# Values of 64-wide heads in two passes, a reordered opening, and projections spread over the heads' turns

## The chip, the cores and the metric

The kernel runs on one core of a Trainium2 chip. The metric is the device time of one execution in microseconds (us): the median of three timed executions. A separate execution was recorded by the hardware profiler; all rows and all times of single instructions here come from it. In the profile PE is the matrix engine TensorE, PEld its weight loads, DVE the vector engine, ACT the scalar engine, POOL the GpSimd engine and SP the engine that issues most loads.

## The reference, cut to what matters

Two transformer blocks run one after the other on a sequence of 512 tokens of width 1024, in float32. The first has two layers (latent attention, then sparse attention, each followed by cross attention and a feed-forward network); the second has forgetting attention beside a pooling mixer, and a convolutional feed-forward network. The change touches the first attention of the first block (16 heads) and the attention of the second block (8 heads). Both have heads of 64 values:

```python
h = x @ w_in                                  # 512 + 256 + 32 columns
q = (rms_norm(c_q, q_norm) @ w_uq)            # per head 64 plain + 32 rotated
kv = (rms_norm(c_kv, kv_norm) @ w_ukv)        # per head 64 key + 64 value
k = concat([k_nope, broadcast(apply_rope(k_rope))])
out = dense_causal_attention(q, k, v, (MLA_NOPE + MLA_ROPE) ** -0.5)
...
s = einsum('bqhd,bkhd->bhqk', qi, k32)        # second block, 8 heads of 64
s = s + Fi[..., None] - Fk[:, :, None, :]
p = softmax(where(qpos >= kpos, s, -inf))
o = einsum('bhqk,bkhd->bqhd', p, v32)
```

## The kernel before, in words

Products keep float32 accuracy by splitting each operand into a high part (rounded to the reduced type fp32r) and a low part (the rest). `split` (lines 157 to 165) makes them with one ACT copy and one DVE subtraction; `mm3` (lines 151 to 155) multiplies high by high, high by low and low by high, three passes on PE into one accumulator. Weights are loaded by SP as "units" in a fixed order (`plan`), and `use` prepares units ahead of their use: ACT makes the high part (L121), and DVE, or POOL during attention, the low part (L122).

**The opening** (`mla`, from line 482). Four tiles of 128 tokens of x are transposed on PE (`tr`, L509) and multiplied by the eight units of the first projection (`front`, 24 pairs of products for each tile, written to `pa` and `pb`). `norm` scales the rows on DVE, `back` transposes them again (L553). SP issues the loads in the order: first halves of x, the first units, then `setup` (nine small loads of constants), then tiles 2 and 3 of x. After the fourth tile the rotated query parts are projected into four accumulators `rq` (two groups of 48 products of 256 columns, one before and one after `back(3, ...)`), rotated by `rope` on DVE (POOL does the products of the later three), values of the first eight heads are projected (`vproj(0)`, four tiles of six products each), and `proj(0)` projects keys (six products) and queries (12 products) of the first two heads. The rotated rows are copied into place by loads on ACT's queue, L622, L623 and L636.

**Attention** (`attention`, lines 672 to 744) runs a loop of turns. In turn h PE multiplies values by probabilities for head h-3 (`s3`, 12 products into `o`), transposes the probabilities of head h-2 (`s2`, ten transposes into three accumulators `t`, which ACT and DVE split into `pt`), and computes the scores of head h (`s1`, 12 products into `s`). DVE subtracts the row maximum and masks (L692), ACT exponentiates (L694); `norm` scales head h-1 on POOL with four instructions (L703). Then `ahead(h)` and `fill(h)` put other PE work into the turn: in even turns the key and query projections of the pair of heads after next (18 products, 4.1 us), in turns 0, 4 and 8 a whole rotation, in turns 1, 3 and 4 the values of the second eight heads (`FILL_V`), and from turn 8 on steps of the cross attention's keys and values (`FILL_A`). Odd turns without a fill have scores, transposes and values alone.

The value product of a head is

```python
o = self.ps("o")
for j in range(NT):
    self.mm3(o[0:64, 128 * j:512], [v[j][:, 0], v[j][:, 1]], [pt[j][:, 0], pt[j][:, 1]], j == 0, j == 3)
self.split(OT[h // 2][r, 0], OT[h // 2][r, 1], o[0:64])
```

with 512, 384, 256 and 128 columns of probabilities for j = 0 to 3 and 64 columns of values as the stationary operand. The second block calls the same `attention` with 8 heads and a lag of 4 turns; there the low parts of weights are made on DVE, and the last four turns have no projection in them.

The order on each engine is a list made before the run, in which an instruction whose inputs are expected early may stand before one that is written earlier. Each engine works through its own list in order.

Of the kernel before, what the change touches and what calls it, by code (L numbers as in the profile page):

```python
# [35 lines left out]
FILL_V = {1: (0,), 3: (1,), 4: (2, 3)}  # L36
# [28 lines left out]
class K:  # L65
# [416 lines left out]
    def mla(self):  # L482
# [3 lines left out]
        for t in range(NT):  # L486
# [8 lines left out]
            if t == 1:  # L495
                self.setup(last)
# [20 lines left out]
        def front(ts, then=None):  # L517
            xT = [x0T.pop(t) if t in x0T else tr(t) for t in ts]
            pp = [(self.ps("pa"), self.ps("pb")) for _ in ts]
            for k in range(8):  # L520
                if len(us) == k:
                    us.append(self.use(3))
                u = us[k]
                for x, (pa, pb) in zip(xT, pp):
                    l = [x[0][:, k], x[1][:, k]]
                    self.mm3(pa, l, [u[0][:, 0:512], u[1][:, 0:512]], k == 0, k == 7)
                    self.mm3(pb[:, 0:288], l, [u[0][:, 512:800], u[1][:, 512:800]], k == 0, k == 7)
                if k == 4 and then is not None:
                    x0T[then] = tr(then)
# [50 lines left out]
        uu = [self.use(), self.use()]  # L580
        for m in range(4):
            rps.append(self.ps("rq"))
        for g in range(2):
            if g == 1:
                back(3, prev)
# [6 lines left out]
            if g == 0:  # L592
                st = {n: self.use() for n in ("v", "k", "q")}
        V = {}

        def vproj(h, js=range(NT)):
            if h == 1 and js[0] == 0:
                st["v"] = self.use()
            u = st["v"]
            for j in js:  # L600
                p = self.ps("v")
                c = slice(j * 128, j * 128 + 128)
                for k in range(2):
                    self.mm3(p, [x[:, c] for x in ckvs[k]], [u[0][:, k], u[1][:, k]], k == 0, k == 1)
                V[h, j] = self.pair("v")
                self.split(V[h, j][:, 0], V[h, j][:, 1], p)

        kr = self.pair("kr")
        self.rope(krf, kr, nc.vector)
# [3 lines left out]
        def ropes(m):  # L613
            rq = self.pair("rq")
            self.rope(rsb[m], rq, nc.vector if m == 0 else nc.gpsimd)
            ropeq.append(rq)
        nc.scalar.copy(rsb[0], rps[0])
        ropes(0)
        for m in range(1, 4):
            nc.scalar.copy(rsb[m], rps[m])  # L620
        for i in range(2):
            nc.scalar.dma_start(KF[i][0][64:96].bitcast(F), kr[64:96].bitcast(F))  # L622
            nc.scalar.dma_start(KF[i][1][32:64].bitcast(F), kr[32:64].bitcast(F))  # L623
        OT = []
        vproj(0)

        def proj(p):
            if p == 4:
                st["k"] = self.use()
            if p in (2, 4, 6):  # L630
                st["q"] = self.use()
            ring = p % 2
            for hd in range(2):
# [3 lines left out]
            for src, nk, w, cc, dst in ((ckvs, 2, st["k"], (p % 4) * 128, KF), (cqs, 4, st["q"], (p % 2) * 128, QF)):  # L637
# [1065 lines left out]
```

## Time and profile before

| | |
|---|---|
| median of three timed executions | 2175.67 us (2175.51 to 2180.46) |
| profiled execution, its time | 2170.42 us |
| its span, first to last instruction | 2168.6 us |
| PE busy | 2125.2 us, 98% of the span |
| DVE, ACT, POOL busy | 61%, 43%, 13% |

Busy shares are means over stages with different limits, so the stages that the change touches are read by themselves below: the opening and first attention (0 to about 230 us of the span) and the second block's attention (about 1677 to 1765 us). A line of the timeline gives the start, the time from start to end, the engine, the line of the kernel, what is written and read, the shape, how many are merged, and in brackets the idle time before it and what ended it. Products on PE overlap, so what one costs is the distance from its start to the next one's start, not its own time.

### The profile page before, as it was taken

Reading aid. Unit: us, or ns where it says so; the run is one execution under the profiler, and the core shown is the slowest. Engines: PE = TensorE matmul, PEld = TensorE weight load, DVE = VectorE, ACT = ScalarE, POOL = GpSimd, SP = SyncE. Lnnn points to the kernel's source line nnn. Section 1 sums busy time; section 2 is a strip of 40 time slices with the busy share of each in tenths; the row PEclk is TensorE's granted clock in tenths of the full one; section 3 lists DMA queues with packets and bytes.
Section 4 is the critical chain, followed back from the end, with each engine's and each line's share of the span. In section 5 each row is a group of like instructions: output and inputs, shape, how many; then the busy total and the mean of one; then the engine's idle time right before and its main releaser. Section 6 shows DMA issues by size and latency. Waiting matters only on the chain.

```text
span 2168.6 us, 30013 instructions
## 1 busy us (share of the span) xinstructions
PE 2125.2 (98%) x11492; PEld 1776.7 (82%) x11492; DVE 1324.1 (61%) x2747; ACT 925.7 (43%) x1684; POOL 287.9 (13%) x288
## 2 busy tenths in 40 slices
PE   8999999999999999899999999999999999999998
PEld 7789898988888887775688888888888879888886
DVE  6776566735237267877676845446377677755734
ACT  3687444313225143578734332224224655343521
POOL 0255100000000002476300000000004310000002
PEclk9999999999999999999999999999999999999999
DMA  6123613355324132240332345444320335432311
GB/s 209 49 67 99 205 59 117 96 167 155 97 94 151 54 107 65 77 123 27 125 119 79 117 155 184 136 127 159 104 59 21 88 112 156 146 94 91 126 59 39
DMA packets 254178, 233.82 MB, mean 108 GB/s; under 512 B 14516, under 2 KB 219700, under 8 KB 254036
## 3 DMA queue, kind: packets, MB, share of 16 engines
q1 hardware_dynamic: 246384, 214.19, 32.1%
q10 hardware_dynamic: 7652, 17.73, 2.6%
q8 instruction: 90, 1.47, 0.3%
q14 instruction: 52, 0.43, 0.1%
HBM read 220.81 MB, written 6.82 MB: 105 GB/s over the span
## 4 chain that ended last, share of the span: by engine, by line
PE 53%; DVE 4%; ACT 2%; issue 1%; POOL 0%; DMA 0%; DVEq 0%; ACTq 0%; POOLq 0%
PE fm L154 9%; PE fm L155 9%; PE fm L153 9%; PE acc L153 6%; PE acc L154 6%; PE acc L155 6%; PE s L1252 1%; PE o L153 1%; PE o L154 1%; PE o L155 1%; DVE sc L1172 1%; PE t L1275 1%; PE v L153 1%; DVE qb L1222 1%; DVE m L1169 1%
## 5 line engine op out<-in xcount | busy, mean ns | idle before, releaser
L154 PE MATMUL fm<-xT,wh 128*128 128x512 f32 (+3 forms) x1640 | 588.8, 361 | 0.4
L155 PE MATMUL fm<-xT,wl 128*128 128x512 f32 (+3 forms) x1640 | 588.3, 359 | 0.0
L153 PE MATMUL fm<-xT,wh 128*128 128x512 f32 (+3 forms) x1640 | 587.7, 360 | 0.5 <-ACT wh L121 0.4
L122 DVE TENSOR_TENSOR wl<-raw,wh 128x1024 fp32r<-128x1024 f32 (+1 forms) x299 | 358.3, 1223 | 94.5 <-ACT wh L121 64.4
L121 ACT CAST wh<-raw 128x1024 fp32r<-128x1024 f32 (+2 forms) x339 | 338.9, 1038 | 71.8 <-PE acc L154 18.8
L154 PEld LDWEIGHTS fm<-xT,wh 128*128 128x128 f32 (+2 forms) x1640 | 307.2, 187 | 48.4 <-DVE xT L250 1.6
L155 PEld LDWEIGHTS fm<-xT,wl 128*128 128x128 f32 (+2 forms) x1640 | 307.4, 187 | 47.2 <-DVE wl L122 0.3
L153 PEld LDWEIGHTS fm<-xT,wh 128*128 128x128 f32 (+2 forms) x1640 | 306.4, 187 | 48.2 <-ACT wh L121 0.9
L122 POOL TENSOR_TENSOR wl<-raw,wh 128x1024 fp32r<-128x1024 f32 (+1 forms) x40 | 93.4, 2344 | 1211.3 <-ACT wh L121 610.6
L153 PE MATMUL acc<-wh,hs 128*128 128x512 f32 x528 | 205.6, 389 | 0.0
L154 PE MATMUL acc<-wl,hs 128*128 128x512 f32 x528 | 205.4, 389 | 0.0
L155 PE MATMUL acc<-wh,hs 128*128 128x512 f32 x528 | 204.9, 389 | 0.0
L974 DVE TENSOR_TENSOR hT<-sil,fm 128x512 f32<-128x512 f32 x44 | 30.3, 688 | 228.5 <-PE fm L155 225.7
L973 ACT ACTIVATE sil<-fm 128x512 f32<-128x512 f32 x44 | 26.3, 598 | 300.6 <-PE fm L155 283.5
L153 PEld LDWEIGHTS acc<-wh,hs 128*128 128x128 f32 x528 | 99.1, 188 | 20.5
L957 DVE SCALAR_TENSOR_TENSOR cv<-fm,cw,cv 128x511 f32<-128x511 f32 x88 | 65.8, 748 | 82.2 <-ACT cv L955 81.0
L154 PEld LDWEIGHTS acc<-wl,hs 128*128 128x128 f32 x528 | 99.1, 188 | 20.5
L155 PEld LDWEIGHTS acc<-wh,hs 128*128 128x128 f32 x528 | 99.1, 188 | 20.5
L153 PE MATMUL acc<-wh,ot 128*128 128x512 f32 x288 | 112.5, 391 | 0.0
L155 PE MATMUL acc<-wh,ot 128*128 128x512 f32 x288 | 112.1, 389 | 0.0
L154 PE MATMUL acc<-wl,ot 128*128 128x512 f32 x288 | 112.1, 389 | 0.0
L217 ACT ACTIVATE x<-x,mv 128x1024 f32<-128x1024 f32 x20 | 24.9, 1243 | 147.9 <-DVE mv L216 147.8
(363 smaller groups left out, 3518.7 us busy)
## 6 DMA issues: line engine op xcount, KB each, us to landing
raw<-in_ffn_w_in_dram SPq DMA_DIRECT2D x88, 512.0 KB
mw<-in_mod_w_dram SPq DMA_DIRECT2D x48, 512.0 KB
raw<-in_ffn_w_down_dram SPq DMA_DIRECT2D x44, 512.0 KB
raw<-in_ffn_up_dram SPq DMA_DIRECT2D x44, 512.0 KB
raw<-in_xa_w_kv_dram SPq DMA_DIRECT2D x32, 512.0 KB
raw<-in_ffn_down_dram SPq DMA_DIRECT2D x22, 512.0 KB
raw<-in_xa_w_q_dram SPq DMA_DIRECT2D x16, 512.0 KB
raw<-in_xa_w_o_dram SPq DMA_DIRECT2D x16, 512.0 KB
```

Source lines behind the costliest of these rows:

```text
L121: self.nc.scalar.copy(hi[:, :n], raw[:, :n])
L122: self.lo_eng.tensor_tensor(lo[:, :n], raw[:, :n], hi[:, :n].bitcast(F), op=OP.subtract)
L153: mm(out, l[0], r[0], start=first, stop=False, **kw)
L154: mm(out, l[0], r[1], start=False, stop=False, **kw)
L155: mm(out, l[1], r[0], start=False, stop=last, **kw)
L217: ops.append(lambda: nc.scalar.activation(x, x, AF.Identity, bias=mv[:, 3:4], scale=mv[:, 2:3]))
L957: nc.vector.scalar_tensor_tensor(y[:, sh:], p[:, :S - sh], w[:, 2 - sh, c:c + 1], y[:, sh:], op0=OP.mult, op1=OP.add)
L973: nc.scalar.activation(s, g, AF.Silu)
L974: nc.vector.tensor_tensor(hT[j // 2][:, j % 2], s, u, op=OP.mult)
L1169: m = v.max(m8, sc[b])
L1172: v.match_replace(sc[b], m8, sc[b], -3.0e38)
L1222: ops.append(lambda o=o, i=i: v.tensor_copy(o, i))
```

## The change

Four things are changed.

1. In both attentions a value tile is stored with its high and low parts side by side for each head (`vsplit`), so one stationary operand of 128 columns holds both. A head takes two passes instead of three for each j: probabilities high and probabilities low, each against both parts. Rows 0 to 63 of `o` then hold the high part's products, rows 64 to 127 the low part's. ACT copies rows 64 to 127 to a scratch tile `y`, DVE adds rows 0 to 63 to it, and the split into `OT` reads `y`. The addition and the split are deferred (`late`): the first behind the transposes of this turn, the second behind the scores.
2. The opening: `setup` goes behind all of x; the first weight unit is used between the transposes of the first two tiles, and the first four steps run as tile 0, tile 0, tile 1, tile 1; units for rotations and values are used before `back(2, ...)`, the next three before the rotations' products; two value tiles (12 products) go ahead of `back(3, ...)`, the other two behind the rotations' start; two value tiles of the second eight heads go behind `proj(0)`; key and first query rotations are interleaved on DVE, and the copies of rotated rows are issued in two parts.
3. In attention, keys are projected in even turns and queries in odd turns, the three later rotations are cut into steps over turns 0 to 9 (`ROPE`), and the value fills shrink to one tile in turns 3 and 4.
4. The load of the small vector `c_2` (before, issued at 1.65 us on ACT's queue) is ordered behind the last activation ahead of the first feed-forward network.

```diff
-FILL_V = {1: (0,), 3: (1,), 4: (2, 3)}
+FILL_V = {3: (2,), 4: (3,)}
+
+ROPE = {0: ((1, 2),), 1: ((1, 2),), 3: ((2, 2),), 4: ((2, 1),), 5: ((2, 1),), 7: ((3, 2),), 8: ((3, 1),), 9: ((3, 1),)}
...
-    def rope(self, src, out, eng):
+    def rope_steps(self, src, out, eng):
...
-        nc.vector.stream_shuffle(t2, src, [(i + 16) % 32 for i in range(32)])
-        eng.tensor_tensor(t1, src, self.cos, op=OP.mult)
-        eng.tensor_tensor(t2, t2, self.sin, op=OP.mult)
-        nc.vector.tensor_tensor(t1, t1, t2, op=OP.add)
-        self.split(out[:, 0], out[:, 1], t1)
+
+        def products():
+            eng.tensor_tensor(t1, src, self.cos, op=OP.mult)
+            eng.tensor_tensor(t2, t2, self.sin, op=OP.mult)
+        return [lambda: nc.vector.stream_shuffle(t2, src, [(i + 16) % 32 for i in range(32)]), products,
+                lambda: nc.vector.tensor_tensor(t1, t1, t2, op=OP.add), lambda: self.split(out[:, 0], out[:, 1], t1)]
...
-            if t == 1:
-                self.setup(last)
+        self.setup(last)
...
-            xT = [x0T.pop(t) if t in x0T else tr(t) for t in ts]
+            xT = []
+            for t in ts:
+                xT.append(x0T.pop(t) if t in x0T else tr(t))
+                if not us:
+                    us.append(self.use(0))
             pp = [(self.ps("pa"), self.ps("pb")) for _ in ts]
...
+            order = [(k, i) for k in range(8) for i in range(len(ts))]
+            if len(ts) == 2:
+                order[:4] = [(0, 0), (1, 0), (0, 1), (1, 1)]
+            for k, i in order:
...
+        self.ahead, self.dma_ahead = 0, 2
+        uu = [self.use(), self.use()]
+        st = {"v": self.use()}
         back(2, scr[2])
         prev = norm(3, *pp[3])
-        self.ahead, self.dma_ahead = 2, 2
+        for n in ("k", "q", "v1"):
+            st[n] = self.use()
+        self.ahead = 2
...
         for g in range(2):
             if g == 1:
+                vproj(0, (0, 1))
                 back(3, prev)
...
+        def ropes(m, n):
+
+            if m not in steps:
+                ropeq.append(self.pair("rq"))
+                steps[m] = self.rope_steps(rsb[m], ropeq[m], nc.gpsimd)
+            for _ in range(n):
+                steps[m].pop(0)()
+
+        def krows(i):
+            nc.scalar.dma_start(KF[i][0][64:96].bitcast(F), kr[64:96].bitcast(F))
+            nc.scalar.dma_start(KF[i][1][32:64].bitcast(F), kr[32:64].bitcast(F))
...
+        ks, qs = self.rope_steps(krf, kr, nc.vector), self.rope_steps(rsb[0], ropeq[0], nc.vector)
+        for x, n in ((ks, 1), (qs, 1), (ks, 2), (qs, 1), (ks, 1), (qs, 2)):
+            for _ in range(n):
+                x.pop(0)()
+        krows(0)
...
-        vproj(0)
-
-        def proj(p):
+        vproj(0, (2, 3))
+
+        def proj(p, which=(0, 1)):
...
         def ahead(h):
-            if h in (0, 4, 8):
-                ropes(h // 4 + 1)
-            if h % 2 == 0 and h < 14:
-                proj(h // 2 + 1)
+            for m, n in ROPE.get(h, ()):
+                ropes(m, n)
+            if h < 14:
+                proj(h // 2 + 1, (h % 2,))
         proj(0)
+        krows(1)
+        vproj(1, (0, 1))
...
+    @staticmethod
+    def hp64(v):
+
+        return v.rearrange("p (a b c) -> p a b c", a=8, b=2)
+
+    def vsplit(self, p):
+
+        v = self.pg(R, "v")
+        x = self.hp64(v)
+        self.split(x[:, :, 0], x[:, :, 1], p.rearrange("p (a c) -> p a c", a=8))
+        return v
...
             for j in range(NT):
-                self.mm3(o[0:64, 128 * j:512], [v[j][:, 0], v[j][:, 1]], [pt[j][:, 0], pt[j][:, 1]], j == 0, j == 3)
+                for i in range(2):
+                    nc.tensor.matmul(o[:, 128 * j:512], v[j], pt[j][:, i], start=j == 0 and i == 0, stop=j == 3 and i == 1)
...
-            self.split(OT[h // 2][r, 0], OT[h // 2][r, 1], o[0:64])
+            y = self.cp.tile([128, 512], F, tag="hp", bufs=3, name=self.nm("oy"))
+            nc.scalar.copy(y[r], o[64:128])
             del A[h]
-
+            return [lambda: nc.vector.tensor_tensor(y[r], o[0:64], y[r], op=OP.add),
+                    lambda: self.split(OT[h // 2][r, 0], OT[h // 2][r, 1], y[r])]
...
             if 0 <= h - 2 < nh:
                 s2(h - 2)
+            if late:
+                late.pop(0)()
             if 0 <= h - 1 < nh:
                 norm(h - 1)
             if h < nh:
                 s1(h)
+            if late:
+                late.pop(0)()
+            if h < nh:
                 ahead(h)
...
-        nc.scalar.dma_start(cc, a["c_2"].rearrange("o (k p) -> p (o k)", p=128))
+        self.after(nc.scalar.dma_start(cc, a["c_2"].rearrange("o (k p) -> p (o k)", p=128)), self.last_act)
```

## Rows read from the trace of the kernel before

**Rows 1.** The page's busy times of the whole span.
```profile
PE 2125.2 (98%) x11492; PEld 1776.7 (82%) x11492; DVE 1324.1 (61%) x2747; ACT 925.7 (43%) x1684; POOL 287.9 (13%) x288
```
**Rows 2.** Windows: stretch, length, busy us per engine (instructions), clock, DMA share, GB/s.
```profile
61.21:70.60 9.39, 9.39 (x61) 8.79 (x61) 8.01 (x13) 4.02 (x7) 0.00 (x0) 0.82 0.01 2
...
80.83:89.42 8.59, 8.28 (x31) 6.57 (x31) 6.52 (x19) 6.17 (x14) 1.30 (x1) 0.80 0.18 49
89.42:120.42 31.00, 31.00 (x185) 26.61 (x184) 24.71 (x65) 25.46 (x62) 18.75 (x20) 1.00 0.11 26
120.42:149.56 29.14, 28.14 (x175) 23.59 (x174) 22.86 (x65) 23.02 (x58) 19.29 (x22) 1.00 0.32 91
149.56:166.46 16.90, 15.59 (x106) 13.58 (x104) 13.29 (x35) 14.21 (x34) 10.45 (x13) 1.00 0.22 55
...
166.46:199.26 32.80, 32.24 (x229) 28.96 (x228) 21.14 (x59) 22.12 (x56) 15.40 (x15) 1.00 0.34 101
...
199.26:230.19 30.93, 30.93 (x222) 28.30 (x221) 16.88 (x30) 20.86 (x37) 19.82 (x14) 1.00 0.51 176
```
**Rows 3.** Timeline of the opening, PE and ACT.
```profile
7.28 0.59 ACT L160 CAST x0T<-tp 128x512 fp32r<-128x512 f32 x1 [0.97 <-PE tp L509]
...
9.91 5.42 ACT L121 CAST wh<-raw 128x800 fp32r<-128x800 f32 x7
...
10.83 0.79 PE L153 MATMUL pa<-wh,x0T 128*128 128x512 f32 x1 [1.43 <-ACT wh L121]
...
24.34 1.07 PE L509 MATMUL tp<-cst,x 128*128 128x128 f32 x8 [0.53 <-DMA x<-in_x_dram]
...
61.21 0.41 PE L553 MATMUL tp<-cst,cn 128*128 128x128 f32 x2 [2.96 <-DVE cn L542]
...
80.83 0.51 PE L689 MATMUL s<-kf,qf 96*128 96x512 f32 x1 [1.66 <-ACT qf L160]
```
**Rows 4.** Timeline of PE: a head's value products; transposes with 128-wide weights.
```profile
146.80 0.40 PE L153 MATMUL o<-pt,v 128*64 128x512 f32 x1
...
147.49 0.33 PE L153 MATMUL o<-pt,v 128*64 128x384 f32 x1
...
148.01 0.28 PE L153 MATMUL o<-pt,v 128*64 128x256 f32 x1
...
148.35 0.22 PE L153 MATMUL o<-pt,v 128*64 128x128 f32 x1
...
148.53 0.29 PE L711 MATMUL t<-cst,P 128*128 128x128 f32 x1
...
153.53 0.71 PE L711 MATMUL t<-cst,P 128*128 128x128 f32 x5
```
**Rows 5.** Groups of ACT and DVE, 80.8 to 199.3 us: busy us, mean ns.
```profile
L160 ACT CAST ot<-o 64x512 fp32r<-64x512 f32 x12 | 7.0, 580 | 4.1 <-PE o L155 3.1 <-DVE rq L161 0.6 <-PE t L711 0.2
...
L160 ACT CAST rq<-rp 128x512 fp32r<-128x512 f32 x3 | 1.9, 621 | 2.3 <-DVE rp L388 1.5 <-DVE st L700 0.7
...
L161 DVE TENSOR_TENSOR ot<-o,ot 64x512 fp32r<-64x512 f32 x12 | 8.1, 678 | 4.7 <-ACT ot L160 4.6
...
L161 DVE TENSOR_TENSOR rq<-rp,rq 128x512 fp32r<-128x512 f32 x3 | 2.1, 686 | 0.0
```
**Rows 6.** Timeline: one DVE operation alone and beside a POOL operation.
```profile
69.39 0.68 DVE L386 TENSOR_TENSOR rp<-krf,trig 128x512 f32<-128x512 f32 x1
...
73.11 1.29 POOL L386 TENSOR_TENSOR rp<-rsb,trig 128x512 f32<-128x512 f32 x1 [28.95 <-ACT rsb L620]
...
73.33 1.61 DVE L386 TENSOR_TENSOR rp<-rsb,trig 128x512 f32<-128x512 f32 x1
```
**Rows 7.** Second block's attention: windows, and PE's longest wait in it.
```profile
1676.80:1725.34 48.54, 48.06 (x248) 39.99 (x249) 31.35 (x74) 30.82 (x72) 15.75 (x20) 1.00 0.29 80
1725.34:1750.35 25.01, 22.22 (x150) 18.24 (x149) 21.33 (x54) 20.67 (x51) 8.27 (x12) 1.00 0.50 165
...
1734.30 0.33 PE L711 MATMUL t<-cst,p 128*128 128x128 f32 x1 [1.38 <-POOL p L703]
```

More of the change, by code (lines that the diff above doesn't have):

```diff
@@ L579, in mla, with vproj @@
         ropeq, rps = [], []
-        uu = [self.use(), self.use()]
         for m in range(4):
             rps.append(self.ps("rq"))
+        V = {}
+        def vproj(h, js=range(NT)):
+            u = st["v1" if h else "v"]
+            for j in js:
+                p = self.ps("v")
+                c = slice(j * 128, j * 128 + 128)
+                for k in range(2):
+                    self.mm3(p, [x[:, c] for x in ckvs[k]], [u[0][:, k], u[1][:, k]], k == 0, k == 1)
+                V[h, j] = self.vsplit(p)
         for g in range(2):
             if g == 1:
+                vproj(0, (0, 1))
                 back(3, prev)
@@ L591, in mla @@
                              [x[:, g * 256:(g + 1) * 256] for x in cqs[k]], k == 0, k == 3)
[L592 to L606, printed above, removed]
@@ L608, in mla @@
         kr = self.pair("kr")
[L609 removed]
         rsb = [self.pg(F, "rsb") for _ in range(2)]
         rsb = [rsb[m // 2][:, (m % 2) * 512:(m % 2) * 512 + 512] for m in range(4)]
[L613 to L616, printed above, removed]
[L617 to L618 removed]
+        steps = {}
+        def ropes(m, n):
[4 more added lines that the diff above has]
+                steps[m].pop(0)()
@@ L619, in mla @@
+        krows(0)
         for m in range(1, 4):
             nc.scalar.copy(rsb[m], rps[m])
-        for i in range(2):
-            nc.scalar.dma_start(KF[i][0][64:96].bitcast(F), kr[64:96].bitcast(F))
-            nc.scalar.dma_start(KF[i][1][32:64].bitcast(F), kr[32:64].bitcast(F))
         OT = []
-        vproj(0)
-        def proj(p):
-            if p == 4:
+        vproj(0, (2, 3))
+        def proj(p, which=(0, 1)):
+            if p == 4 and 0 in which:
                 st["k"] = self.use()
-            if p in (2, 4, 6):
+            if p in (2, 4, 6) and 1 in which:
@@ L631, in proj @@
                 st["q"] = self.use()
             ring = p % 2
-            for hd in range(2):
+            for hd in range(2 if 0 in which else 0):
                 h = 2 * p + hd
@@ L636, in proj @@
                 nc.scalar.dma_start(QF[ring][hd][rows].bitcast(F), ropeq[h // 4][32 * (h % 4):32 * (h % 4) + 32].bitcast(F))
-            for src, nk, w, cc, dst in ((ckvs, 2, st["k"], (p % 4) * 128, KF), (cqs, 4, st["q"], (p % 2) * 128, QF)):
+            for i in which:
+                src, nk, w, cc, dst = ((ckvs, 2, st["k"], (p % 4) * 128, KF), (cqs, 4, st["q"], (p % 2) * 128, QF))[i]
                 q = self.ps("qk")
@@ L664, in fill @@
             self.fill(FILL_A.get(h, 0))
-        self.attention(16, rowsel, lambda h: [V[h // 8, j][:, :, (h % 8) * 64:(h % 8) * 64 + 64] for j in range(NT)],
+        self.attention(16, rowsel, lambda h: [V[h // 8, j][:, (h % 8) * 128:(h % 8) * 128 + 128] for j in range(NT)],
                        OT, scale, ahead,
@@ L1480, in second @@
         for j in range(NT):
-            V.append(self.pair("v"))
-            self.split(V[j][:, 0], V[j][:, 1], vp[j])
+            V.append(self.vsplit(vp[j]))
         QF, KF = [], []
@@ L1540, in pools @@
                 pool_mm(g, mps[g], pw[0])
-        self.attention(8, rows, lambda h: [V[j][:, :, h * 64:h * 64 + 64] for j in range(NT)], OT, 1.0, before,
+        self.attention(8, rows, lambda h: [V[j][:, h * 128:h * 128 + 128] for j in range(NT)], OT, 1.0, before,
                        fill=pools, lag=4)
```

16 lines of the change are left out of this document (8 added, 8 removed).

## The prediction

> **What bounds the kernel now.** I read the page's busy times first: PE is busy 98% of the span [rows 1], so taking work from PE should show, but only in stages where PE and not a dependency sets the pace. So I cut the first attention into stretches of turns, from the first score product of one head to that of another [rows 2]. Three kinds appear. In turns 1 to 4 (89.42:120.42) PE is busy all 31.00 us, DVE 24.7, ACT 25.5. In turns 5 to 10 PE is idle 1.0 of 29.14 and 1.3 of 16.90 us; these gaps lie in the odd turns, which have no projection. In turns 11 to 14 and behind them PE is nearly always busy. DVE and ACT are busy 78 to 84% of turns 1 to 10, close behind PE; the reader is to remember this, because the change moves work onto both.
>
> Then the opening's timeline [rows 3]. PE starts its first projection product at 10.83 us, released by ACT's weight copy; it waits 0.53 us for tile 2 of x, 2.96 us for `norm` before `back(3)`, and 1.66 us for the query split before the first scores. The granted clock is 1.00 in the other windows, but a mean of 0.82 behind the 2.96 us wait and 0.80 behind the 1.66 us one [rows 2]: part of each stretch ran at 1.2 instead of 2.4 GHz. That cost 9.39 x 0.18 = 1.7 us and 8.59 x 0.20 = 1.7 us of PE time. In the second block PE is busy 48.06 of 48.54 us while projections run, and 22.22 of 25.01 us in the last turns, where it waits for POOL's `norm` [rows 7].
>
> **The value products.** Three passes over 512, 384, 256 and 128 columns take, start to start, 0.69 + 0.52 + 0.34 + 0.18 = 1.73 us a head, 0.577 us a pass [rows 4]. One pass goes. The stationary operand grows from 64 to 128 columns, and the trace of before has no such product in this place. Above: nothing more, saving 0.577 us. Below: the 128-column passes go at the pace of the transposes, which have 128-wide weights and 128 columns: five span 0.71 us and one lasts 0.27 to 0.29, so (0.71 - 0.27)/4 = 0.11 instead of 0.06 [rows 4]; two of them lose 0.10, saving 0.48. These shapes are nearest, so I take 0.50 us a head. The Trainium skill (TensorE: Matmul & The Clock Gate, LDWEIGHTS) says a load takes the columns over 1.2 GHz, thus 107 ns for 128; by that estimate the two short passes lose about 0.05 us each, which would make it 0.48 us a head and 0.5 us less in the whole sum.
>
> The price is off PE: an ACT copy like the 580 ns one, and a DVE addition like the 678 ns subtraction, for each head; the split that follows has the old shapes and reads `y` where it read `o` (621 and 686 ns at the same length where both inputs are in working memory) [rows 5]. Starts lie some 0.1 us closer than ends, so about 0.6 us each on ACT and DVE. The accumulator `o`, one of eight, is freed by the addition, behind the subtractions of `pt` where the old split stood before them; PE takes it again a turn later. Behind the addition on DVE stand the reciprocal for POOL's `norm` and the maxima of the next scores; behind the copy on ACT stand the splits of `pt` and the exponentials. These are hidden only while PE is the slowest.
>
> **The opening.** The first weight copy comes after two `x0T` copies instead of four, thus at 7.28 + 0.59 = 7.9 us; at 5.42/7 = 0.77 us a copy [rows 3] the first product can start at 8.7, 2.1 us earlier. If the clock rises no earlier than before, half of that is lost. With the 0.53 us wait for x gone (tiles 2 and 3 now pass nine small loads on SP's queue, whose first reader, `norm`, stands behind all products of the first two tiles) I get 1.6 to 2.6, and take 2.2 us. The 2.96 us wait is filled by 12 value products, 12 x 0.23 = 2.8 us [rows 4], so the clock should hold. From `back(3)` to the first scores took 80.83 - 61.21 = 19.6 us for 15.9 us of PE work (seven transposes at 0.11; 48 products of 256 columns at 0.113; 24 and 18 of 512 at 0.23). The work after the change is the same sum (12 value products gone ahead, 12 of the second eight heads added). If no clock loss and no wait remain, 3.7 us are won; if the wait for rotated rows and query splits stays at 1.66, 2.1. I take 2.9. The opening's sum is 5.1 us, bounds 3.7 and 6.3.
>
> **The turns of the first attention** [rows 2].
> - Turn 0, 8.59 us: the query projection (12 x 0.23 = 2.8) leaves it and the 1.7 us of slow clock go: 4.5 won.
> - Turns 1 to 4, 31.00 us, PE-bound: 12 value products (2.8) are now done ahead of the scores, three heads save 1.5: PE needs 26.7; DVE needs 24.7 + 3 x 0.6 less two value splits, some 25.3. I take 27.2: 3.8 won.
> - Turns 5 to 8, 29.14 us: PE 28.14 - 4 x 0.5 = 26.1; DVE 22.86 and ACT 23.02 get 4 x 0.6, thus 25.3 and 25.4. Spreading gives each turn 1.4 or 2.7 us of cover, but three engines with 25.3 to 26.1 us each will not mesh fully: halfway between 26.1 and 29.14 is 27.6: 1.5 won.
> - Turns 9 and 10: ACT is fullest, 14.21 + 1.2 = 15.4 of 16.90; halfway is 16.1: 0.8 won.
> - Turns 11 to 14: four heads save 2.0, the projection moved out of turn 0 returns (2.8), the idle 0.56 is covered: about -0.2.
> - Behind them (199.26:230.19, PE always busy): three heads save 1.5.
>
> Sum: 11.9 us. Bounds: if turns 5 to 10 win nothing and turns 1 to 4 only the 2.8, 8.6; if PE alone counts at 0.577 a head (turns 1 to 4 in 26.5, 5 to 8 in 25.8, 9 and 10 in 14.4), 16.6.
>
> **The second block.** Two heads fall in the part where PE is full: 1.0 us. In the last turns PE waits for POOL, so a shorter product wins nothing and the deferred operations may lengthen the chain. I take 0.5; bounds -2.5 and +3.5.
>
> **The rest at nothing.** The rotations cut into steps and the value units used earlier are the same instructions in other places. The copies of key rows are still four, two of them behind `proj(0)` on ACT's queue; they feed the third head, a turn later. The `c_2` load is hidden by the feed-forward network's products; uncovered it would cost the landing of a 4 KB load.
>
> Sum: 5.1 + 11.9 + 0.5 = 17.5 us. The profiled execution is 2170.4 us (span 2168.6 and 1.8 around it) and lies 5.3 below the median 2175.7; the gain comes off either, so I forecast 2175.7 - 17.5 = **2158.2 us**.
>
> **The rivals.**
> - *DVE and ACT become the bound.* Every head adds 0.6 us to two engines that were busy 78 to 84% of turns 1 to 10. For it speaks that odd turns already waited for ACT and DVE; against it, that PE was full in turns 1 to 4. Then attention wins only 8.6 - 2.5 (queries projected in the odd turn are split just before the next scores, some 0.35 us late in each of seven) = 6.1, the second block loses 1: 5.1 + 6.1 - 1 = 10.2, time 2165. Chance 0.22.
> - *PE alone counts.* Spreading removes all waits: 6.3 + 16.6 + 3.5 = 26.4, time 2149. Against it: three engines over 93% full. Chance 0.13.
> - *Slower: DVE and POOL get in each other's way.* The deferred subtraction reads two operands in working memory (`y` and the high part) where the old one read the accumulator. A DVE product with two such operands took 0.68 us alone and 1.61 when it started during a POOL operation [rows 6]: 0.93 lost. POOL is busy 63% of turns 1 to 10 [rows 2]. If every deferred subtraction meets POOL and POOL's `norm` waits 0.69 in turn, both on the path, 24 x 1.62 = 39 us are lost, time 2197. It cancels the gain from 17.5/24 = 0.73 us a head. Against it: `norm` is mostly covered by other PE work, and the subtraction's result isn't needed for many turns. Chance 0.06. The Trainium skill (SBUF — State Buffer, SBUF: two separate sides) states it as a rule: a vector operation with two such inputs and GpSimd exclude one another for a whole instruction. The trace agrees in the one collision above.
> - *The change does not do what it says*: the fixed lists place the deferred pieces and filled-in products elsewhere, waits move, and only the shorter products in full stretches remain (about nine heads, 4.5 us), or a new wait eats them: 2170 to 2179. Chance 0.08.
>
> **How the numbers follow.** The forecast's own case (2153 to 2163) has 0.51, the others 0.22, 0.13, 0.06 and 0.08. A range from 2147 to 2169 takes in the first two rivals and leaves out the last two and little more. A measurement of this kernel tells about 0.3% (6.5 us) from no change: faster means below 2169.2. The forecast, the PE-only case and most of the first rival lie there: 0.84; same 0.11; slower 0.05.
>
> **What would show it.** Value products 128 wide, 8 a head, 1.15 to 1.26 us; the first projection product near 8.7 us; no granted clock below 1.00 between the opening's end and turn 0; first scores near 75.7 us; turns 5 to 8 in 27 to 28 us; 199.26's place reached 15 to 16 us earlier. It would be wrong if even turns wait for `qf`, if turns follow DVE at over 95% busy, or if subtractions from `y` last over 1 us.

## The result, and the profile after

The kernel became slower: median 2192.11 us against 2175.51, ratio 1.0086 (95% interval 1.0069 to 1.0103). The forecast was 2158.2. A ratio isn't the quotient of the two medians, so the two differ a little. Line numbers are each kernel's own. The profiled execution has a span of 2199.0 us. It is the slowest of the change's five executions (2200.79 us against a median of 2192.11), and the profiled one before was faster than all timed ones, so the two traces lie 30.4 us apart where the medians lie 16.6. This is the page's row of busy times, beside [rows 1]:

```profile
PE 2139.0 (97%) x11396; PEld 1792.7 (82%) x11396; DVE 1345.9 (61%) x2770; ACT 939.8 (43%) x1708; POOL 292.8 (13%) x289
```

PE runs 96 fewer products and is busy 13.8 us longer. The windows after, cut like those of [rows 2] from one head's first score product to another's, tell why (columns as there; the last ends at the first product of the output projection, which before stood at 244.92 us):

```profile
62.97:81.76 18.79, 18.79 (x97) 16.74 (x98) 13.11 (x24) 7.61 (x16) 1.83 (x1) 0.85 0.16 36
81.76:85.06 3.30, 3.30 (x19) 2.91 (x18) 2.19 (x7) 3.24 (x7) 0.00 (x0) 1.00 0.18 40
85.06:130.54 45.48, 35.23 (x162) 28.73 (x160) 27.97 (x74) 27.33 (x67) 24.60 (x24) 0.77 0.19 52
...
130.54:162.47 31.93, 29.22 (x160) 25.49 (x157) 27.48 (x68) 25.28 (x62) 17.93 (x19) 0.89 0.28 84
162.47:179.25 16.78, 15.04 (x98) 13.17 (x95) 14.39 (x37) 14.57 (x37) 7.60 (x11) 1.00 0.18 47
179.25:218.92 39.67, 35.93 (x224) 33.20 (x223) 27.29 (x65) 26.34 (x62) 18.75 (x18) 0.91 0.30 87
218.92:263.05 44.13, 44.13 (x276) 39.96 (x273) 29.35 (x43) 29.72 (x50) 19.83 (x14) 1.00 0.55 187
```

| stretch | before, us | after, us | forecast | measured |
|---|---|---|---|---|
| up to the first scores | 80.83 | 81.76 | -5.1 | +0.9 |
| turn 0 | 8.59 | 3.30 | -4.5 | -5.3 |
| turns 1 to 4 | 31.00 | 45.48 | -3.8 | +14.5 |
| turns 5 to 8 | 29.14 | 31.93 | -1.5 | +2.8 |
| turns 9 and 10 | 16.90 | 16.78 | -0.8 | -0.1 |
| turns 11 to 14 | 32.80 | 39.67 | +0.2 | +6.9 |
| behind them | 45.66 | 44.13 | -1.5 | -1.5 |

The sum is 18.1 us. Of the other 12.3 us between the two traces, 10.3 lie between the output projection and the second block's first scores (1442.2 us against 1431.9), a stretch whose instructions the change leaves alone but for the `c_2` load; the last experiments come back to it. The `c_2` load isn't the reason: ACT waits 2.5 us for it, but from 240 to 600 us, where it now stands, PE is busy 359.84 of 360 us, as before.

In turns 1 to 4 PE is idle 10.3 us and the clock's mean is 0.77, where before PE was never idle and the clock stayed at 1.00 [rows 2]. PE's longest waits between 48 and 219 us (engine, what is written, who came last, total, times, longest):

```profile
PE qk L155 <- ACT wh L123: 5.1, 1, 5.1
PE tp L561 <- DVE cn L550: 5.0, 1, 5.0
PE k L157 <- POOL wl L124: 3.2, 1, 3.2
PE qk L157 <- POOL wl L124: 2.7, 1, 2.7
PE s L724 <- ACT qf L162: 2.6, 3, 1.9
```

Four of the five end in a weight unit's preparation: three directly (`wh`, `wl`), one, `cn`, by what stands ahead of it on DVE. The timeline of the opening, beside [rows 3]:

```profile
8.91 0.78 PE L155 MATMUL pa<-wh,x0T 128*128 128x512 f32 x1
...
57.63 1.23 DVE L124 TENSOR_TENSOR wl<-raw,wh 128x1024 fp32r<-128x1024 f32 x1
58.78 0.15 DVE L186 SCALAR_TENSOR_TENSOR ss<-rs,ss 128x2 f32<-128x2 f32 x1
58.85 1.22 DVE L124 TENSOR_TENSOR wl<-raw,wh 128x1024 fp32r<-128x1024 f32 x1
...
60.05 1.22 DVE L124 TENSOR_TENSOR wl<-raw,wh 128x1024 fp32r<-128x1024 f32 x1
...
62.97 1.11 PE L561 MATMUL tp<-cst,cn 128*128 128x128 f32 x4 [4.99 <-DVE cn L550]
```

The subtractions of the `k`, `q` and `v1` units stand on DVE's list between `norm`'s small operations (0.15 us each), 3.7 us in sum, and `norm` releases `back(3)` that much later. And turn 3, which took 6.16 us before and 19.25 now:

```profile
110.50 2.94 ACT L123 CAST wh<-raw 128x1024 fp32r<-128x1024 f32 x3
110.74 2.88 POOL L738 TENSOR_TENSOR P<-P,st 128x512 f32<-128x512 f32 x2
111.60 0.79 PE L155 MATMUL qk<-cq,wh 128*128 128x512 f32 x1 [5.13 <-ACT wh L123]
...
113.58 2.33 POOL L124 TENSOR_TENSOR wl<-raw,wh 128x1024 fp32r<-128x1024 f32 x1
...
115.97 0.79 PE L157 MATMUL qk<-cq,wl 128*128 128x512 f32 x1 [2.73 <-POOL wl L124]
```

The query unit of the third pair is cast when its product is already due, behind the exponentials, and its low part waits on POOL behind `norm`. Before, `ahead` (how many units are prepared in advance) was 2 in the opening and this unit was ready long ago; now it is 0 there until the `v1` unit is used. Behind the first wait the starts of products are 0.43 us apart instead of 0.23, and the granted clock from 111.60 to 119.50 us is 0.50: PE runs at 1.2 GHz.

The value products themselves came out as forecast. Eight of them and the transpose behind, beside [rows 4]:

```profile
149.29 1.37 PE L760 MATMUL o<-pt,v 128*128 128x512 f32 x8
150.50 0.29 PE L746 MATMUL t<-cst,P 128*128 128x128 f32 x1
```

That is 1.21 us a head, 0.52 less than 1.73. The Trainium skill's load time (TensorE: Matmul & The Clock Gate, LDWEIGHTS) had given 0.48 by estimate; the trace decides for 0.52. In the second block the stretch from the first scores to the eighth head's grew from 58.46 to 61.91 us, with one wait of 2.7 us for a transpose behind DVE; from the first scores to the end of the kernel the profiled execution lost 2.0 us.

### The profile page after: what moved, and what is told of

Read it like the earlier page. It is cut to its first block, busy times and chain, and to the rows that moved or that the text cites. A ratio compares the mean times of both kernels' runs of the same rounds, so it can differ in the third digit from the quotient of the medians.

```text
span 2199.0 us, 29854 instructions
## 1 busy us (share of the span) xinstructions
PE 2139.0 (97%) x11396; PEld 1792.7 (82%) x11396; DVE 1345.9 (61%) x2770; ACT 939.8 (43%) x1708; POOL 292.8 (13%) x289
## 4 chain that ended last, share of the span: by engine, by line
PE 85%; DVE 8%; ACT 4%; issue 2%; POOL 1%; DMA 1%; SPq 0%; ACTq 0%; DVEq 0%; POOLq 0%
PE fm L156 14%; PE fm L155 14%; PE fm L157 14%; PE acc L156 9%; PE acc L155 9%; PE acc L157 9%; PE v L155 1%; PE v L156 1%; PE v L157 1%; PE s L1297 1%; PE o L155 1%; PE o L156 1%; DVE pt L163 1%; ACT P L729 1%; PE s L724 1%
```

## Experiments

Numbers are medians in us; the ratio is to the kernel before on the same chip (its medians there 2174.87 to 2175.51), with its 95% interval. The last column is the trace's: how much later than before (244.92 us) PE starts the output projection, so where opening and first attention have ended. Each trace is of one execution. In e5, f1 and f2, whose opening is that of the kernel before, the first scores come 0.2 to 1.1 us later than before and turn 1 begins 1.6 to 2.1 us later, so this column can't tell less than about 2 us.

| kernel | median | ratio | attention ends |
|---|---|---|---|
| the change | 2192.1 | 1.0086 (1.0069 to 1.0103) | +18.1 |
| e1_prep | 2186.0 | 1.0049 (1.0032 to 1.0065) | +7.7 |
| e2_norm | 2191.5 | 1.0073 (1.0054 to 1.0091) | +13.7 |
| e3_both | 2181.5 | 1.0030 (1.0019 to 1.0040) | +10.1 |
| e4_both_nospread | 2185.0 | 1.0055 (1.0035 to 1.0076) | +10.4 |
| e5_before_values | 2183.3 | 1.0040 (1.0027 to 1.0053) | +10.8 |
| f1_nofold | 2178.4 | 1.0014 (1.0005 to 1.0023) | +0.7 |
| f2_psum | 2183.3 | 1.0041 (1.0028 to 1.0054) | +6.9 |
| f3_open | 2186.2 | 1.0049 (1.0036 to 1.0063) | +10.1 |
| f4_open_spread | 2189.9 | 1.0063 (1.0047 to 1.0078) | +17.8 |
| g1_open_mended | 2174.1 | 0.9995 (0.9985 to 1.0005) | -0.6 |
| h3_open_cover | 2175.6 | 0.9999 (0.9989 to 1.0008) | -2.4 |
| h7_two | 2180.8 | 1.0026 (1.0015 to 1.0037) | +6.3 |
| h6_two_lag4 | 2181.8 | 1.0026 (1.0015 to 1.0036) | +1.2 |
| f6_front | 2171.0 | 0.9982 (0.9974 to 0.9990) | -2.9 |
| f7_front_mixed | 2177.3 | 1.0005 (0.9995 to 1.0015) | -3.4 |
| h4_shift4 | 2176.4 | 1.0004 (0.9993 to 1.0014) | -1.8 |
| h1_shift | 2177.6 | 1.0007 (0.9999 to 1.0016) | +1.1 |
| h2_shift20 | 2178.8 | 1.0015 (1.0005 to 1.0025) | +1.9 |

**Units late (e1, e2, e3).** e1 prepares the next query unit ahead of the attention; e2 orders the three subtractions behind `norm`; e3 does both.

```diff
         vproj(1, (0, 1))
+        self.ensure(self.cur + 1)            # e1, e3
...
+        self.behind_norm = self.last_split   # e2, e3
         for n in ("k", "q", "v1"):
             st[n] = self.use()
+        self.behind_norm = None
...
+        if self.behind_norm is not None:
+            self.after(low, self.behind_norm)
```

> One line is added to the changed kernel: the query weights of the third pair of heads are split ahead of the attention, with the low part on DVE, instead of in turn 3. T1 (work that used to be prepared ahead is now asked for on demand, and each wait of PE is followed by a stretch at 1.2 GHz): turn 3 falls from 19.25 to 9 to 11 us, the stretch at half clock near 110 to 120 us goes, and the time falls from 2192 to 2182 to 2185. R1 (ACT and DVE are the bound): the same casts are only moved, the sum over turns 0 to 10 falls by less than 3 us, time 2189 to 2192. R2 (queries in odd turns make the scores wait): turns 7 and 9 stay as they are, and so does most of the loss, 2188 or more.

> In the changed kernel the three weight subtractions on DVE are ordered behind the last operation of the fourth tile's norm. T1: PE's wait ahead of the fourth back falls from 5.0 us to 1.3 us or less and the half clock behind it goes or shrinks, so the first scores come at 76 to 78 us instead of 81.8, time 2186 to 2189. Rival: the subtractions are late for the value products behind them, the wait moves there, the first scores stay at 81 to 82 and the time at 2192.

> Both edits in the changed kernel: the query unit of the third pair prepared ahead, and the three subtractions behind the norm. T1: the two gains add, 12 to 15 us, time 2177 to 2181, about the kernel before; what is then missing to the forecast (2158) lies in turns 1, 2, 7, 8 and 11. R1 (ACT and DVE bound): 2188 or more. R3 (the deferred subtraction collides with POOL): its mean stays near 965 ns and costs 12 heads x 0.28 us = 3.4 us on DVE, not more.

e1 brought turn 3 from 19.25 to 8.36 us, the last column from +18.1 to +7.7, and the median down by 6.1 us: the unit's share is shown. e2 brought the wait from 5.0 to 1.9 us, but a wait of 1.6 us for the split of `cq` followed, because the subtractions now stood ahead of it; the first scores came at 81.94. The rival held for e2 alone. Together they won 10.6 of the 16.6 us in the median; e3 still loses 6.6 to the kernel before on its chip. In the traces e3 ends its attention 2.4 us later than e1, and takes 7.5 us less from there to the second block's scores (1432.8 against 1440.3), where the two kernels do not differ. So what e3 has over e1 in the median isn't shown to be the second mend's.

**Two passes alone (e5), without their price (f1), without the collision (f2).** e5 is the kernel before with `vsplit`, the two-pass products, `y` and the deferred pieces. f1 drops the copy and the addition, so its output lacks the products of the values' low part. f2 adds into the accumulator:

```diff
-    return [lambda: nc.vector.tensor_tensor(y[r], o[0:64], y[r], op=OP.add),
-            lambda: self.split(OT[h // 2][r, 0], OT[h // 2][r, 1], y[r])]
+    return [lambda: nc.vector.tensor_tensor(o[0:64], o[0:64], y[r], op=OP.add),
+            lambda: self.split(OT[h // 2][r, 0], OT[h // 2][r, 1], o[0:64])]
```

> The kernel before with the two-pass values alone, in both attentions: old opening, old projections, old rotations. T1: with the old cover the shorter products pay where PE is full, some 12 of 24 heads at 0.5 us, time 2166 to 2172. R1 and R3 (the price on ACT and DVE, or the collision with POOL, eats them): turns 1 to 10 no shorter than 77 us, time 2175 to 2185.

> The kernel before with the two-pass values alone, and without the copy and the addition: the split takes rows 0 to 63 of the accumulator as before, so the products of the low part of the values are left out of the output. It has PE's saving and none of the price. Price theory (the copy, the addition and the split behind them make PE wait on DVE and ACT): the loss of the two-pass values alone (+8.4 us) turns into a gain of 6 to 12 us, time 2163 to 2169, and turns 4, 5 and 9 are no longer than before. Rival (the wide products themselves, or the shorter cover on PE, make the waits): it stays at 2178 to 2184, and turns 5 and 9 still take 9 to 10 us. In between, both have a share.

> The kernel before with the two-pass values alone, but the addition writes back to the accumulator and the split reads it there, so that the subtraction no longer has two inputs in working memory; as many operations as with y. Collision theory (R3, the subtraction from y stands still beside POOL): its mean falls from about 900 ns to 0.69 us, turns 4, 5 and 9 lose most of their excess, time 2172 to 2177. Rival (the mere number and order of operations on DVE and ACT): 2181 to 2186.

My theory fell here: with all the old cover, two passes lose 8.4 us. e5's timeline shows how, in turns 4, 8 and 9:

```profile
111.90 1.33 DVE L161 TENSOR_TENSOR ot<-oy,ot 64x512 fp32r<-64x512 f32 x1 [0.33 <-ACT ot L160]
...
113.16 0.67 DVE L161 TENSOR_TENSOR v<-v,v 128x512 fp32r<-128x512 f32 x1
...
113.88 0.50 PE L153 MATMUL qk<-ckv,wh 128*128 128x512 f32 x1 [1.82 <-DVE v L161]
...
154.21 1.54 DVE L161 TENSOR_TENSOR ot<-oy,ot 64x512 fp32r<-64x512 f32 x1
...
156.40 0.68 DVE L161 TENSOR_TENSOR kf<-qk,kf 64x512 fp32r<-64x512 f32 x1
...
159.22 0.69 DVE L161 TENSOR_TENSOR kf<-qk,kf 64x512 fp32r<-64x512 f32 x1
...
160.06 0.59 PE L700 MATMUL s<-kf,qf 128*128 128x256 f32 x3 [1.56 <-DVE kf L161]
```

The deferred subtraction, whose result nobody needs for many turns, stands on DVE ahead of the value split that frees PE's next accumulator, and ahead of the keys' split for the next scores. In turn 4 of the kernel before, the two stand the other way round, and PE doesn't wait there:

```profile
109.97 0.69 DVE L161 TENSOR_TENSOR v<-v,v 128x512 fp32r<-128x512 f32 x1 [0.29 <-ACT v L160]
110.69 0.68 DVE L161 TENSOR_TENSOR ot<-o,ot 64x512 fp32r<-64x512 f32 x1
```

In turns 5 and 9 of e5 PE waits and slows down, and turn 6 pays for turn 5: PE never waits in it, and runs at a mean clock of 0.68.

```profile
123.06:132.29 9.23, 6.85 (x34) 4.82 (x32) 7.95 (x20) 6.49 (x17) 4.45 (x6) 0.85 0.53 145
132.29:144.12 11.83, 11.83 (x51) 10.21 (x49) 6.55 (x17) 8.35 (x19) 6.18 (x8) 0.68 0.05 12
156.75:167.28 10.53, 5.16 (x27) 4.10 (x25) 8.46 (x21) 6.58 (x14) 3.88 (x5) 0.83 0.05 12
```

Turn by turn the saving is there where PE is full: turns 2, 8, 11, 12 and 13 of e5 are 0.5 us shorter each than before, and the part behind the last turn 1.5 (44.14 us against 45.66). Turns 4, 5, 6, 9 and 10 lose 14.4 us together.

Without the price (f1) turn 9 is back at 6.19 us (6.29 before), turn 5 at 8.02 (5.80 before):

```profile
121.94:129.96 8.02, 6.32 (x34) 5.42 (x32) 6.09 (x17) 4.56 (x14) 2.75 (x4) 0.81 0.43 107
152.19:158.38 6.19, 4.80 (x34) 4.10 (x32) 5.96 (x16) 3.54 (x9) 3.07 (x4) 1.00 0.19 44
```

So the price costs 4.9 us in the medians (10 in the traces' last column). Free of charge the shorter products win little. f1's trace starts turn 1 2.1 us later than before and the output projection 0.7 later, so in between, where the products are, it wins 1.4 us of the 8.3 that 16 heads at 0.52 could give. In turn 5 PE waits 1.4 us for POOL's `p` and then runs below full speed. The median is 2.9 us up all the same, but the trace has its loss where nothing was edited: 1439.3 us instead of 1431.9 between the output projection and the second block's scores. f2 removes the collision and doesn't move the median (its one trace is 3.9 us shorter). The groups of the subtraction in e5 and in f2, from 80 to 245 us (busy us, mean ns):

```profile
L161 DVE TENSOR_TENSOR ot<-oy,ot 64x512 fp32r<-64x512 f32 x16 | 14.4, 903 | 0.6 <-ACT ot L160 0.3
```

```profile
L161 DVE TENSOR_TENSOR ot<-o,ot 64x512 fp32r<-64x512 f32 x16 | 10.9, 681 | 0.8 <-ACT ot L160 0.6
```

The subtraction with two inputs in working memory takes 0.22 us more than the one with an input in the accumulator. The Trainium skill (SBUF — State Buffer, SBUF: two separate sides) says that a DVE operation with two SBUF inputs and a GpSimd operation that reads SBUF shut one another out for a whole instruction; both rows agree. These 0.22 us a head aren't the cause, since taking them away left the median where it was. What remains is the number of the added pieces and their place in the lists; no run tells these two apart.

**The opening and the spreading (f3, f4, e4, g1, h3).** f3 is the change with three passes and old projections (a pair's keys and queries in one even turn, whole rotations), f4 the change with three passes only, e4 is e3 with old projections. g1 mends f3: the three units are used behind `back(3)`, and the query unit ahead. h3 also puts the second values back.

```diff
-        for n in ("k", "q", "v1"):
-            st[n] = self.use()
-        self.ahead = 2
...
                 back(3, prev)
+                for n in ("k", "q", "v1"):
+                    st[n] = self.use()
+                self.ahead = 2
...
-        vproj(1, (0, 1))                     # h3 alone
+        self.ensure(self.cur + 1)
...
-FILL_V = {3: (2,), 4: (3,)}                  # h3 alone
+FILL_V = {1: (0,), 3: (1,), 4: (2, 3)}
```

> The changed kernel with three-pass values and with a pair's projections in one even turn and whole rotations again: what is left of the change is the opening. T1: the first projection product stays at 8.9 us and the front end 3 us early, but the wait ahead of the fourth back and the half clock behind it eat it, and the query unit prepared on demand costs 3 to 8 us in turn 2: 2176 to 2183. Rival (the opening is a gain, only values and spreading lose): 2169 to 2173.

> The changed kernel with three-pass values: opening and spreading without the two-pass values. If the values' price is what loses, it is 6 to 10 us under the changed kernel: 2182 to 2186. If the missing cover loses (T1), longer value products fill part of the waits, 2184 to 2189. If spreading is the gain it was taken for, it is faster than the opening alone by 2 us or more.

> The changed kernel with both edits (query unit of the third pair ahead, the three subtractions behind the norm), and without the spreading: a pair's projections in one even turn, whole rotations in turns 0, 4 and 8. If spreading is a gain once its units are ready (keys in one turn, queries in the next give every turn cover), this is 3 us or more slower than the 2181.5 of the same kernel with spreading. If spreading itself costs (queries split just before the next scores, more pieces on DVE), it is 3 us or more faster. Within 3 us: spreading is worth nothing either way.

> The opening alone (three passes, a pair's projections in one even turn) with two edits: the key, query and value units are used behind the fourth back instead of ahead of it, so that their subtractions stand neither in the norm nor ahead of the query rows' split, and the query unit of the third pair is prepared ahead of the attention. T1: the wait ahead of the fourth back falls to 1.5 to 2 us, turn 2 from 19.1 to 9 us, first scores at 77 to 80 us, time 2170 to 2176. Rival (the opening's order itself loses, whatever is prepared when): 2180 or more.

> The mended opening (2174.1), with the second eight heads' values in turns 1, 3 and 4 as in the kernel before, and none ahead of the scores; three passes, no spreading. Theory (what the opening won was given back in turns 1 and 2 for lack of PE work that covers the first norm): first scores near 72 us, turn 1 at 4.3 us instead of 7.9, turn 2 at 8.9 instead of 12.1, 2167 to 2170. Rival (the start of the pipeline waits for norm whatever stands in turn 1): turns 1 and 2 keep 18 us or more in sum, 2173 or above.

The opening as it stands loses 10.7 us, more than I had expected: the same wait of 5.0, and 19.1 us in turn 2 for the unit on demand. Mended (g1), the wait for `cn` is gone, the clock stays at 1.00 up to the first scores, and these come at 74.55 us, 6.3 us earlier than before; the prediction had 75.7. The 6.3 us are given back: turn 1 has no values left as cover, PE waits 2.5 us for POOL's `P`, and turns 0 to 4 run at 0.88. h3 gives the cover back and ends its attention 2.4 us before the kernel before, little more than such a trace can tell; I had expected 2167 to 2170 us, and it stayed at 2175.6. Its scores don't come earlier for the 12 products taken out ahead of them (74.46 us, PE waits 2.5 us there for the query split), and turn 3 waits 1.1 us for DVE. Windows from the first scores to turn 5 in g1 and in h3:

```profile
74.55:117.77 43.22, 39.48 (x203) 32.91 (x203) 30.66 (x81) 31.27 (x74) 20.00 (x21) 0.88 0.18 46
```

```profile
74.46:117.68 43.22, 40.65 (x214) 33.07 (x215) 31.44 (x82) 32.12 (x75) 19.98 (x21) 0.96 0.18 46
```

Before, turns 0 to 4 took 39.59 [rows 2]. Neither median differs from before. Spreading is worth 3.5 us in the medians (e4 against e3), but 0.3 in the traces' last column; 2.4 lie in the unedited stretch behind it (1435.3 against 1432.8). It shortens turn 9 from 10.52 to 7.39 and lengthens turn 11 from 10.06 to 17.92, where 2.7 us are the query projection and 3.2 a wait for the cross attention's unit on POOL. Without mends it cost 3.7 (f4 against f3). The prices of opening, values and spreading taken alone (10.7, 8.4 and 3.7 us) sum to 22.8, more than the 16.6 of the change: they overlap.

**Two passes on the mended opening (h7), with a turn more for the chain (h6).** h6 passes `lag=4`.

> The mended opening with its cover, two passes for all values, and the value products of the first attention one turn later (a lag of 4 turns instead of 3). Theory (the two-pass values lose because the chain of one head through ACT, DVE and POOL no longer fits into the shorter turns): with one more turn PE's waits for pt go from turns 5, 7 and 9, and it is as fast as the same opening with three passes or up to 4 us faster. Rival (the added pieces on ACT and DVE delay norm and the projections' splits themselves): 5 us or more slower than three passes, with waits for P and for qf in turns 5 and 9.

> As the last, with the lag of 3 turns: the best opening with the two-pass values as they are. By the earlier pair (two passes alone on the kernel before: 8.4 us slower) 5 to 9 us slower than the same opening with three passes. If it is faster, the loss of two passes came from the old opening's place, not from the attention.

Two passes lose 5.2 us here too. The further turn wins 5 us in the trace and nothing in the median, and turn 9 still waits 1.9 us for the keys' split and 2.7 for `P`: the rival fits better. But h6's trace is of the fastest of its 12 executions (2175.0 us against a median of 2181.8) and h7's is not, so the two can't be compared by it, and the further turn's worth stays open.

**The front alone (f6), and two passes where PE is full (f7).**

> The kernel before with the first half of the new opening alone: small loads behind all of x, the first unit used between the first two tiles, the first four steps in the order tile 0, 0, 1, 1. The prediction's own term (2.2 us for this part): first projection product at 8.7 to 8.9 us, first scores 2 to 3 us earlier, 2172 to 2173.5. Rival (the gain is waited away ahead of the fourth back, since norm and trigonometry on DVE and ACT are not earlier): first scores as before, 2175 to 2176.

> The same, and two passes for the values of seven heads of the first attention (7 to 9 and 12 to 15, whose products stand in turns 10 to 12 and behind the last turn, where keys and values of the cross attention cover the chain) and of the second block's first head; three passes for all others. Theory (a shorter product pays where other work of PE fills the turn, and nowhere else): 8 heads x 0.5 = 4 us under the kernel with the new front alone, 2168 to 2170. Rival (the price on ACT and DVE loses here too): as much as the new front alone or more, 2172 or above.

f6 beats both kernels in the median: first scores at 77.95, 2.9 us earlier (forecast for this part: 2.2). That isn't one lucky trace: the five kernels with this front (f6, f7, h1, h2, h4) have them at 77.95 to 78.72 us, the four with the old opening (the kernel before, e5, f1, f2) at 80.83 to 81.94. f7 ends its attention 0.5 us earlier still, and is 6.3 us slower. In its trace the two passes win 1.5 us behind the last turn, as in e5, and lose 1.2 in turn 10, which takes 11.82 us instead of 10.60 and in which PE is idle for 1.0. In the profiles the loss lies between the output projection and the second block's scores (1442.8 us against 1434.9), in the sparse attention, whose instructions stand in the same order on every engine in f6, f7 and the change. That led to the last test.

**A mere shift (h1, h2, h4).** f6 with 10, 20 and 4 products on PE behind the first attention:

```diff
+        z = self.ps("z")
+        for i in range(10):
+            nc.tensor.matmul(z, OT[7][:, 0, 0:128], OT[0][:, 0], start=i == 0, stop=i == 9)
```

> The kernel with the new front alone (2171.0), and ten more products of 512 columns on PE behind the first attention (10 x 0.23 = 2.3 us), whose result nothing reads; every other engine's list is the same. If the later stages cost the same wherever they start: 2173.3, within 1 us. If the sparse attention's clock depends on when it is reached (its instructions stand in the same order in all kernels, but it had 10 to 34 us at 1.2 GHz in the profiles): 2175 to 2180, or below 2172, with more than 13.6 us or fewer at half clock in it.

> The kernel with the new front alone and twenty instead of ten extra products (4.5 us) behind the first attention. If each shift has its own clock in the sparse attention: anything from 2174 to 2184, and not 4.5 us above 2171.0 within 1 us. If the ten products cost 6.6 us for another reason than the shift (a price for each product): 2171.0 + 13 = 2184. If the stage costs the same and the ten were an accident: 2175.5.

> The same with four extra products, 0.9 us. If the stage costs the same wherever it starts: 2171.9. By a price for each product as the ten had it: 2173.6. If the clock of the sparse attention follows the shift: either of these or up to 2178, and the profile shows it in the us at 1.2 GHz between 890 and 1010 us.

0.9, 2.3 and 4.5 us of products cost 5.4, 6.6 and 7.8 (2176.4, 2177.6 and 2178.8 against f6's 2171.0): each 3 to 5 us more than itself. By the ratios, which allow for the different chips, it is 4.8, 5.4 and 7.2. Windows of the sparse attention in f6, then with 4, 10 and 20 products (last column but two: mean clock):

```profile
890.00:1010.00 120.00, 108.12 (x1047) 82.79 (x1047) 92.78 (x303) 89.23 (x256) 75.14 (x80) 0.94 0.26 78
```

```profile
890.00:1010.00 120.00, 107.45 (x977) 84.61 (x976) 84.83 (x279) 81.13 (x232) 69.69 (x75) 0.86 0.26 79
```

```profile
890.00:1010.00 120.00, 107.82 (x998) 84.00 (x996) 88.89 (x287) 84.96 (x241) 72.38 (x76) 0.89 0.28 87
```

```profile
890.00:1010.00 120.00, 109.37 (x1037) 85.48 (x1035) 90.16 (x304) 88.37 (x251) 75.86 (x79) 0.91 0.29 90
```

These clocks are of one execution each, and they don't rank the cost. From the output projection to the second block's scores f6 takes 1434.9 us; with 4, 10 and 20 products it is 1442.9, 1438.9 and 1434.9. Executions of one kernel differ as much: h4's 12 lie between 2169.85 and 2180.31 us, f6's between 2170.08 and 2174.46. So the added products have no fixed price, and why they lengthen the median isn't shown. The stretch took 1431.9 to 1442.9 us over all traces, and `c_2` has no part in it: kernels with its new place have 1432.8 to 1442.2, kernels without 1431.9 to 1442.9.

So an attribution by medians is good to some 4 us, and 1.3 of f6's 4.2 us, if not more, are not the front's: 0.9 us of added products take its lead away.

## Why the prediction was wrong

1. The step that failed is "The rest at nothing", with its "the value units used earlier are the same instructions in other places". They were the same instructions; their places were inside `norm`(3) and behind a due product. Preparation on demand cost 6.1 us in the median (e1; 10.9 in turn 3 of the trace), and both unit mends together won back 10.6 of the 16.6 (e3, with what is said there of its median). A unit on demand in turn 11 cost another wait of 3.2 us, which is in e3 too. The other term at nothing, the `c_2` load, was right: PE doesn't wait for it.
2. "The 2.96 us wait is filled by 12 value products, so the clock should hold" counted the filling, not what came with it: the products filled the gap, and `norm` came later by the three subtractions put into it; the wait was 4.99 us. With the units moved (g1) the clock held and the first scores came at 74.55, so the opening's sum could be reached: 6.3 us, its upper bound.
3. The value products' saving was right in size (0.52 for 0.50) and wrong in what it was worth. I counted 1.5 us of it in turns 1 to 4 and half of what there was in turns 5 to 10; alone, it lost 8.4 (e5); without its price it won 1.4 us of the first attention's 8.3 in the trace, and the median was 2.9 up (f1). "These are hidden only while PE is the slowest" was the condition. It held in turns 2, 8, 11, 12 and 13 and behind the last turn, where e5 has the 0.5 us a head. In turns 4, 5 and 9 the shorter PE work came back as waits, and in turns 5, 6, 9 and 10 as 1.2 GHz.
4. The price (0.6 us a head on ACT and on DVE) was about right: by the page's rows the change has ACT busy 14.1 and DVE 21.8 us longer, 0.59 and 0.91 a head, and on DVE 0.2 to 0.3 of it is the collision (0.22 a head in e5), far below the rival's 1.62. What was left out is the order: a deferred piece stands ahead of splits that PE waits for (e5's turns 4 and 9). The first rival had the two engines as the bound and still forecast a gain (2165); in e5 the same price ended in a loss.
5. Turn 0 (-5.3, forecast -4.5) and the part behind the last turn (-1.5) came about as forecast: PE is never idle in either.
6. The fourth rival ("waits move, or a new wait eats them", 2170 to 2179) named the mechanism and ended short of it, since it counted waits without the stretch at half clock behind them. The bound of "PE alone counts" contradicts the prediction's own sums: it puts turns 9 and 10 at 14.4 us, where the bullet on them has ACT busy for 15.4.

What stays open: what a lag of 4 turns is worth to two passes, whether number or place of the added pieces costs more, and how much of each median is the later stage's.

## What to carry to other kernels

Before a product is shortened, list for each turn what PE would then wait for; the saving is real only in turns that keep other ready work. When uses of prepared weights move, write down for each unit the engine, the queue position and the time of its cast and subtraction, as for any new instruction. A deferred operation needs a place behind everything that PE waits for, not only a late one in the program; no run here tried that place. Before a gain of a few us is given to an edit, compare the stages that it doesn't touch.

## What the runs showed that I had not expected

A wait costs more than its length. Behind the long waits of the change PE ran at 1.2 GHz for some time (mean clocks 0.85, 0.77, 0.89 and 0.91 in the windows above): turn 3 took 10.9 us more than with the same work in e1 (19.25 against 8.36), for 7.9 us of waits. The price can also fall in a turn without any wait, as in e5's turn 6 (11.83 us instead of 8.86).

And the stretch behind the first attention, with the same instructions, took 8 us longer in h4's trace than in f6's (1442.9 us against 1434.9), with mean clocks of 0.86 and 0.94 in its sparse attention. The Trainium skill (TensorE: Matmul & The Clock Gate, Part 1: The HAM clock gate) says that the number of slow products at a kernel's start varies from run to run. No run here was made to show that.
